# Attention stage of an encoder trunk: projection weights issued from GpSimd's queue, key weights split one unit ahead

## The chip, the cores and the metric

The kernel runs on one core of a Trainium2 chip. The metric is the device time of one execution in microseconds; the time before is the median of three runs, 4154.11 us (4153.01 to 4157.19). A core has TensorE (PE; its weight loads are shown apart as PEld), VectorE (DVE), ScalarE (ACT), GpSimd (POOL) and SyncE (SP). Each engine works through its own list of instructions in order. SyncE, ScalarE and GpSimd can also issue DMA transfers, and a transfer that has to wait for something holds up whatever stands behind it on the engine that issues it.

## The reference

The reference is a trunk of two layers over 1280 tokens (256 of a prompt, 1024 of a sample, the latter a grid of 16 by 64), with 1024 channels. Layer 0 mixes tokens by a bidirectional recurrence, layer 1 by neighbourhood attention, and each is followed by a squared-ReLU MLP. The change acts in layer 1's attention:

```python
qkv = (h @ w_qkv).reshape(B, rows, GRID_W, 3, N_HEADS, HEAD_DIM)
q = _rms_norm(qkv[:, :, :, 0], q_g) * (HEAD_DIM ** -0.5)
k = _rms_norm(qkv[:, :, :, 1], k_g)
v = qkv[:, :, :, 2]
...
s = jnp.einsum('bhcqd,bhrcsd->bhcqrs', q_i, k_s).astype(jnp.float32)
s = s + jnp.transpose(bias, (0, 2, 3, 1, 4)).astype(jnp.float32)
s = jnp.where(col_mask[:, :, None, :], s, -jnp.inf)
p = jax.nn.softmax(s, axis=(-2, -1)).astype(v_s.dtype)
o = jnp.einsum('bhcqrs,bhrcsd->bhcqd', p, v_s)
```

Each query of the grid sees a window of 8 rows and 16 columns around it, with a bias table per head (the random inputs are scaled, which changes nothing in the work done). There are 16 heads of 64 channels.

## The kernel before

All data are 32-bit. To keep precision, each matmul operand is split into a rounded high part and the remainder, and every product is made of three matmuls (`mm3`, lines 96 to 98: high by high, low by high, high by low). `wsplit` (line 81) does this for a weight: a DMA brings a piece into the buffer `raw` (line 89), ScalarE rounds it into `whi` (line 90, a CAST), and GpSimd subtracts to get `wlo` (line 91). For the attention's query and key weights `w_nq` and `w_nk` the piece is half a weight block, 128 partitions by 512 numbers (256 KB), and there is one `raw` buffer for both, so that a half can be fetched only after the half ahead of it has been subtracted. `whi` and `wlo` have two buffers each, one for keys and one for queries in turn.

The attention stage works in eight units m, a unit being 128 channels (two heads). `qk_proj(m)` makes a list of small work items: load the weights, then for keys (which = 1) and queries (which = 0) and for each of three token segments eight `mm3` items, an evacuation from PSUM (`evac`: for queries `sq` and `qf`, lines 1595 and 1597, followed by the casts `qs`), and a tiny matmul for the norm (`nst`, line 1612). The key norm is spread over the tokens by transposes `pb` (line 1647), which take turns with the projections in the two PSUM buffers "ps", so that a `pb` must wait until an earlier result, `qf`, has been evacuated. `attend(m)` gives ten steps of attention, each with three parts: scores on TensorE with the softmax on VectorE, ScalarE and GpSimd (the maximum and reciprocal `mx` at lines 1807 and 1809, the exponential at 1808, the multiply at 1810), transposes `pt` with their copy back (lines 1817 and 1818), and the product with the values (`op`, line 1875).

`attend_all` runs the steps of unit m and spreads the work items of unit m + 1 between them, so that projections fill TensorE while the softmax of a step is under way; unit 0's items are worked off ahead of the first step. TensorE's order is this written order. On the other engines, and on the queues of SyncE and GpSimd, a scheduler fixes the order when the program is built.

Other transfers in the stage: the bias tables `bs` and `bpm` of the next unit (lines 1763 and 1769, SyncE; they wait until VectorE has read the present ones), the values `vs` (line 1752, SyncE; those of unit 0 from GpSimd), and the stores of finished outputs `at_d` (line 1776, GpSimd). At the end `output_operands` loads the first weights `w_no` of the output projection through the same `raw` buffer, from SyncE.

Of the kernel before, what the change touches and what calls it, by code (L numbers as in the profile page):

```python
# [49 lines left out]
class Trunk:  # L50
# [27 lines left out]
        return self.vec[:, base + i:base + i + 1]  # L78


    def wsplit(self, pool, src, n, lo_eng, tag="w", hb=2, rb=2, cuts=1):
        nc = self.nc
        hi = pool.tile([P, n], F32R, name="whi", tag=tag + "h", bufs=hb)
        lo = pool.tile([P, n], F32R, name="wlo", tag=tag + "l", bufs=hb)
        w = n // cuts
        for c in range(0, n, w):
            cs = slice(c, c + w)
            raw = pool.tile([P, w], F32, name="raw", tag=tag + "r", bufs=rb)
            nc.sync.dma_start(raw, src[:, cs])
            nc.scalar.copy(hi[:, cs], raw)  # L90
            lo_eng.tensor_tensor(out=lo[:, cs], in0=raw, in1=hi[:, cs].bitcast(F32), op=ALU.subtract)  # L91
        return hi, lo
# [1464 lines left out]
    def qk_proj(self, m):  # L1557


        nc, a, act = self.nc, self.a, self.act  # L1560
        J = {}
        work = []

        def load():
            for nm in ("ks0", "ks1", "qs0", "qs1", "ql"):
                J[nm] = self.qke[m % 2].tile([P, T], F32R, name=nm, tag=nm, bufs=1)
            for e in range(2):
                J["qs", e], J["ks", e] = J[f"qs{e}"], J[f"ks{e}"]
            J["st"] = self.apn.tile([P, 2, 10, 2], F32, name="nst", tag="nst")
        late = []  # L1570
        for which, wname, g in ((1, "w_nk", self.vec[:, V_KG:V_KG + 1]), (0, "w_nq", self.gq)):
            def wload(wname=wname, which=which):
                J["w", which] = self.wsplit(self.awp, a[wname][m], 1024, nc.gpsimd, rb=1, cuts=2)
            work.insert(1 - which, wload)
            for s, (c0, c1) in enumerate(SEGS):
                n = c1 - c0
                R = {}

                def mm(k, R=R, which=which, n=n, c0=c0, c1=c1):
                    if k == 0:  # L1580
                        R["ps"] = self.apd.tile([P, 512], F32, name="ps", tag="ps")
                    hi, lo = J["w", which]
                    self.mm3(R["ps"][:, :n], hi[:, k * P:(k + 1) * P], lo[:, k * P:(k + 1) * P],
                             act[k][0][:, c0:c1], act[k][1][:, c0:c1], k == 0, k == KT - 1)

                def evac(R=R, which=which, g=g, n=n, c0=c0, c1=c1):
                    ps = R["ps"][:, :n]
                    R["sq"] = self.awk.tile([P, 512], F32, name="sq", tag="sq", bufs=3)
                    sv = R["sq"][:, :n]
                    if which == 0:  # L1590

                        qf = self.awk.tile([P, 512], F32, name="qf", tag="sq", bufs=3)
                        sv = sv.rearrange("p (b r w) -> p r b w", b=4, w=16)
                        ps = ps.rearrange("p (r b w) -> p r b w", b=4, w=16)
                    nc.scalar.activation(sv, ps, AF.Square)
                    if which == 0:
                        nc.scalar.activation(qf[:, :n].rearrange("p (b r w) -> p r b w", b=4, w=16), ps, AF.Copy, scale=g)
                        for e in range(2):
                            es, eo = slice(64 * e, 64 * e + 64), slice(64 - 64 * e, 128 - 64 * e)
                            qe = J["qs", e][:, c0:c1]  # L1600
                            nc.scalar.copy(qe[es], qf[es, :n])
                            nc.vector.tensor_tensor(out=J["ql"][es, c0:c1], in0=qf[es, :n], in1=qe[es].bitcast(F32), op=ALU.subtract)
                            (nc.scalar.copy, nc.vector.tensor_copy)[e](qe[eo], qf[es, :n])
                    else:

                        kh, kl = J["ks1"][:, c0:c1], J["ks0"][:, c0:c1]
                        nc.scalar.activation(kh, ps, AF.Copy, scale=g)
                        nc.vector.scalar_tensor_tensor(out=kl, in0=ps, scalar=g, in1=kh.bitcast(F32), op0=ALU.mult, op1=ALU.subtract)

                def stat(R=R, which=which, n=n, c0=c0):  # L1610
                    for b in range(n // P):
                        nc.tensor.matmul(J["st"][:, which, c0 // P + b, :], R["sq"][:, b * P:(b + 1) * P], self.blk, start=True, stop=True)
                for k in range(KT):
                    work.append(lambda k=k, f=mm: f(k))
                    if k == 2 and late:
                        work.extend(late)
                        late = []
                work.append(evac)
                late.append(stat)
            if which == 1:  # L1620
                def spread(s):
                    c0, c1 = SEGS[s]
                    nb = (c1 - c0) // P
                    re = J["re", s] = self.awk.tile([P, 4, P], F32, name="re", tag="re", bufs=2)
                    rk = J["rs", 1][:, c0 // P:c1 // P, :]
                    nc.vector.tensor_copy(re[:, :nb, :].rearrange("p b (h c) -> p b h c", h=2), rk.unsqueeze(3).to_broadcast([P, nb, 2, 64]))

                def norm(which=which):
                    rs = self.awp.tile([P, 20], F32, name="rs", tag="rs", bufs=4)
                    x = self.awk.tile([P, 40], F32, name="rqx", tag="rqx", bufs=2)  # L1630
                    nc.vector.scalar_tensor_tensor(out=x[:, :20].rearrange("p (b h) -> p b h", h=2), in0=J["st"][:, which], scalar=1.0 / 64,
                                                   in1=self.tn[:, 2 - which].unsqueeze(2).to_broadcast([P, 10, 2]), op0=ALU.mult, op1=ALU.add)
                    self.rsqrt_x(x, self.awk, 20, rs)
                    J["rs", which] = rs.rearrange("p (b h) -> p b h", h=2)
                    if which == 1:
                        spread(0)
                        spread(1)
                late.append(norm)
                kn = norm

        ks = []
        for s, (c0, c1) in enumerate(SEGS):
            def kscale(s=s, c0=c0, c1=c1):
                nb = (c1 - c0) // P
                pb = self.apd.tile([P, 512], F32, name="pb", tag="ps")
                for b in range(nb):
                    nc.tensor.transpose(pb[:, b * P:(b + 1) * P], J["re", s][:, b, :], self.ident)
                if s == 0:
                    spread(2)
                k_ = self.awk.tile([P, 512], F32, name="kf", tag="sq", bufs=3)[:, :c1 - c0]  # L1650
                nc.vector.tensor_tensor(out=k_, in0=J["ks1"][:, c0:c1].bitcast(F32), in1=J["ks0"][:, c0:c1].bitcast(F32), op=ALU.add)
                nc.vector.tensor_tensor(out=k_, in0=k_, in1=pb[:, :c1 - c0], op=ALU.mult)

                for e in range(2):
                    es, eo = slice(64 * e, 64 * e + 64), slice(64 - 64 * e, 128 - 64 * e)
                    ke = J["ks", e][:, c0:c1]
                    nc.scalar.copy(ke[es], k_[es])
                    nc.gpsimd.tensor_tensor(out=ke[eo], in0=k_[es], in1=ke[es].bitcast(F32), op=ALU.subtract)
            ks.append(kscale)
        work.insert(2, load)  # L1660
        n = len(work)
        for i, f in enumerate(ks):
            work.insert(n - 17 + 5 * i, f)
        work += [lambda: None] * 2 + late + [lambda: kn(0)]
        return J, work
# [295 lines left out]
```

## Time and profile before

| | |
|---|---|
| median of 3 runs | 4154.11 us (4153.01 to 4157.19) |
| profiled execution | 4156.58 us, span 4154.6 us |
| mean granted TensorE clock | 0.957 |
| the stage's units, between 2675.5 and 3071.5 us | six, 62.2 to 69.1 us each |
| TensorE busy in these six | 363.0 of 396.0 us |
| GpSimd busy in these six | 173.7 of 396.0 us |

In rows of the trace, "out<-in" names what an instruction writes and reads, and the brackets at a row's end give the idle time of the engine ahead of it and what ended it. "ACT whi L90" is the instruction of line 90 on ScalarE that writes `whi`. A row of waits reads: who waited for whom, the sum in us, how many times, the longest. For a DMA the row with three numbers gives minimum, median and maximum. SPq is SyncE's queue.

### The profile page before, as it was taken

The page shows a single profiled execution, that of the slowest core. Times are in us where ns is not written, and L with a number is a line of the kernel's source. Part 1 is how long each engine was busy: PE and PEld are TensorE (multiplying, and loading weights), DVE is VectorE, ACT ScalarE, POOL GpSimd, SP SyncE. Part 2 cuts the span into 40 slices and gives each one's busy share as a digit, 9 for nine tenths or more (in the row PEclk, how much of TensorE's full clock was granted, in tenths as well). Part 3 has the DMA queues.
Part 4 walks back from the last instruction along what each step waited for, and adds up shares of the span by engine and source line. Part 5 has one row for each costly group of instructions (what it writes and reads, how often), then busy time and mean ns, then how long its engine had stood idle before and what let it go on. Part 6 is the DMA issues. An engine that isn't in the chain of part 4 may idle for free.

```text
span 4154.6 us, 86991 instructions
## 1 busy us (share of the span) xinstructions
PE 3837.0 (92%) x35188; PEld 3233.9 (78%) x35188; DVE 2459.8 (59%) x4771; ACT 1547.9 (37%) x3731; POOL 1262.3 (30%) x1210
## 2 busy tenths in 40 slices
PE   7897879688889799999999989899989999999999
PEld 4664669688888688888888879777767788888887
DVE  7888973466666447555555560566664655555555
ACT  6776651354555431111111132555554211112111
POOL 5440000123323434222222240344453422222222
PEclk9997889899999899999999999999999999999999
DMA  3325555866765331111111125333343111111101
GB/s 111 89 95 203 195 189 151 203 175 176 184 172 139 122 114 36 32 41 41 37 36 41 41 73 169 73 84 73 69 117 129 47 41 41 36 36 41 41 31 61
DMA packets 385794, 393.22 MB, mean 95 GB/s; under 512 B 161872, under 2 KB 306480, under 8 KB 384112
## 3 DMA queue, kind: packets, MB, share of 16 engines
q1 hardware_dynamic: 331760, 315.16, 27.1%
q10 hardware_dynamic: 46704, 61.35, 4.3%
q0 software_dynamic: 6928, 11.15, 1.0%
q8 instruction: 276, 4.52, 0.5%
q14 instruction: 126, 1.03, 0.1%
HBM read 277.54 MB, written 121.24 MB: 96 GB/s over the span
## 4 chain that ended last, share of the span: by engine, by line
PE 72%; DVE 13%; issue 4%; ACT 4%; DMA 4%; POOL 2%; SPq 1%; ACTq 0%; DVEq 0%; POOLq 0%
PE ps L96 17%; PE ps L97 17%; PE ps L98 17%; PE by L998 3%; PE bx L998 3%; PE kps L960 2%; PE vps L512 1%; PE vps L513 1%; PE vps L514 1%; PE zps L1166 1%; PE op L1875 1%; DVE cs L628 1%; PE pt L1817 1%; PE aps L833 1%; PE yps L922 1%
## 5 line engine op out<-in xcount | busy, mean ns | idle before, releaser
L1432 DVE TENSOR_TENSOR x<-ps,x 128x256 f32<-128x256 f32 x1488 | 813.6, 594 | 638.8 <-PE ps L98 638.3
L96 PE MATMUL ps<-ah,whi 128*128 128x512 f32 (+1 forms) x2304 | 846.6, 367 | 5.5 <-ACT whi L90 5.0
L98 PE MATMUL ps<-ah,wlo 128*128 128x512 f32 (+1 forms) x2304 | 826.8, 359 | 2.5 <-POOL wlo L91 2.3
L97 PE MATMUL ps<-al,whi 128*128 128x512 f32 (+1 forms) x2304 | 826.7, 359 | 0.0
L91 POOL TENSOR_TENSOR wlo<-raw,whi 128x1024 fp32r<-128x1024 f32 (+1 forms) x178 | 390.6, 2195 | 864.3 <-ACT whi L90 836.8
L96 PE MATMUL ps<-hh,whi 128*128 128x512 f32 (+1 forms) x1536 | 547.7, 357 | 14.3 <-DVE x L1432 14.3
L97 PE MATMUL ps<-hl,whi 128*128 128x512 f32 (+1 forms) x1536 | 545.9, 355 | 0.0
L98 PE MATMUL ps<-hh,wlo 128*128 128x512 f32 (+1 forms) x1536 | 545.9, 355 | 0.0
L96 PEld LDWEIGHTS ps<-ah,whi 128*128 128x128 f32 x2304 | 437.4, 190 | 84.7 <-issue 13.0
L98 PEld LDWEIGHTS ps<-ah,wlo 128*128 128x128 f32 x2304 | 436.6, 189 | 73.9 <-POOL wlo L91 3.4
L97 PEld LDWEIGHTS ps<-al,whi 128*128 128x128 f32 x2304 | 437.2, 190 | 65.4 <-issue 1.1
L90 ACT CAST whi<-raw 128x1024 fp32r<-128x1024 f32 (+1 forms) x206 | 200.6, 974 | 712.7 <-PE ps L97 640.5
L96 PEld LDWEIGHTS ps<-hh,whi 128*128 128x128 f32 x1536 | 291.2, 190 | 59.2 <-DVE x L1432 17.4
L1411 POOL TENSOR_TENSOR rl<-rl 128x512 f32<-128x512 f32 (+1 forms) x192 | 173.9, 906 | 504.0 <-PE ps L98 463.3
L98 PEld LDWEIGHTS ps<-hh,wlo 128*128 128x128 f32 x1536 | 291.4, 190 | 41.8
L97 PEld LDWEIGHTS ps<-hl,whi 128*128 128x128 f32 x1536 | 291.4, 190 | 40.9
L1410 ACT ACTIVATE rl<-ps 128x512 f32<-128x512 f32 (+1 forms) x192 | 100.4, 523 | 547.9 <-PE ps L98 547.9
L965 DVE TENSOR_TENSOR zz<-kps,cst 128x512 f32<-128x512 f32 x160 | 110.3, 690 | 207.7 <-ACT ll L970 207.6
L1413 ACT CAST hh<-rl 128x512 fp32r<-128x512 f32 (+1 forms) x192 | 105.5, 549 | 321.3 <-POOL rl L1411 321.2
L1414 DVE TENSOR_TENSOR hl<-rl,hh 128x512 fp32r<-128x512 f32 (+1 forms) x192 | 119.3, 621 | 150.2 <-ACT hh L1413 149.9
L1810 POOL TENSOR_TENSOR s<-s,mx 128x384 f32<-128x384 f32 (+1 forms) x154 | 116.8, 769 | 212.6 <-DVE mx L1809 148.1
L960 PE MATMUL kps<-x 64*64 64x128 f32 (+1 forms) x2560 | 167.9, 320 | 13.2 <-issue 12.1
(313 smaller groups left out, 7869.0 us busy)
## 6 DMA issues: line engine op xcount, KB each, us to landing
x<-x_d SPq DMA_DIRECT2D x88, 512.0 KB, 4.5
raw<-in_w_down_dram SPq DMA_DIRECT2D x64, 512.0 KB, 3.5
raw<-in_w_up_dram SPq DMA_DIRECT2D x64, 512.0 KB, 3.5
eab<-x_d SPq DMA_DIRECT2D x80, 256.0 KB, 6.0
x_d<-ar ACTq DMA_DIRECT2D x32, 512.0 KB, 3.3
x_d<-bk ACTq DMA_DIRECT2D x32, 512.0 KB, 4.3
bs<-tab SPq DMA_DIRECT2D x128, 96.0 KB, 3.7
v_d<-vt ACTq DMA_DIRECT2D x80, 128.0 KB, 3.7
```

What stands on the lines that cost most here:

```text
L90: nc.scalar.copy(hi[:, cs], raw)
L91: lo_eng.tensor_tensor(out=lo[:, cs], in0=raw, in1=hi[:, cs].bitcast(F32), op=ALU.subtract)
L96: mm(ps, sh, mh, start=first, stop=False)
L97: mm(ps, sh, ml, start=False, stop=False)
L98: mm(ps, sl, mh, start=False, stop=last)
L960: mm(J["kp"][out, e, 192 * c + 192 - w:192 * c + 192], x[es, b, 2 * pr + c], x[es, 5 - w // 64:5, 2 * pr + c], start=True, stop=True)
L965: nc.vector.tensor_tensor(out=z, in0=src[:, :, :, :P], in1=self.mask[d].unsqueeze(1).unsqueeze(1).to_broadcast([P, 2, 2, P]), op=ALU.mult)
L998: mm = lambda out, a, b, start, stop: nc.tensor.matmul(out, a, b, start=start, stop=stop, skip_group_check=True)
L1411: nc.gpsimd.tensor_tensor(out=r[:, :n], in0=r[:, :n], in1=r[:, :n], op=ALU.mult)
L1414: nc.vector.tensor_tensor(out=hl[:, :n], in0=r[:, :n], in1=hh[:, :n].bitcast(F32), op=ALU.subtract)
L1432: nc.vector.tensor_tensor(out=xv, in0=ps[:, :n], in1=xv, op=ALU.add)
L1810: nc.gpsimd.tensor_tensor(out=s[:, :nk], in0=s[:, :nk], in1=mx[:, 2:3].to_broadcast([P, nk]), op=ALU.mult)
```

## The change

`wsplit` gets an argument for the engine that issues its transfers. In `qk_proj` the key and query weights of units 1 to 7 come from GpSimd's queue; unit 0's stay on SyncE. The key weights of unit m + 1 become an item of unit m's list, between its key and its query projections (`wnext`), and unit m takes the pair made there. The query weights of units 1 to 7 are loaded behind the first four key matmul items instead of at the list's start, and the allocation of the unit's tiles (`load`) moves to the front of the list.

```diff
-    def wsplit(self, pool, src, n, lo_eng, tag="w", hb=2, rb=2, cuts=1):
+    def wsplit(self, pool, src, n, lo_eng, tag="w", hb=2, rb=2, cuts=1, dma=None):
...
-            nc.sync.dma_start(raw, src[:, cs])
+            (dma or nc.sync).dma_start(raw, src[:, cs])
...
-            def wload(wname=wname, which=which):
-                J["w", which] = self.wsplit(self.awp, a[wname][m], 1024, nc.gpsimd, rb=1, cuts=2)
-            work.insert(1 - which, wload)
+            def wload(wname=wname, which=which, m=m):
+                J["w", which] = self.wsplit(self.awp, a[wname][m], 1024, nc.gpsimd, rb=1, cuts=2, dma=nc.gpsimd if m else None)
+
+            def wnext():
+                self.wnext = self.wsplit(self.awp, a["w_nk"][m + 1], 1024, nc.gpsimd, rb=1, cuts=2, dma=nc.gpsimd)
+            if m == 0:
+                work.insert(1 - which, wload)
+            elif which == 1:
+                J["w", 1] = self.wnext
+            else:
+                work.insert(4, wload)
+            if which == 0 and m < 7:
+                work.append(wnext)
...
-        work.insert(2, load)
+        work.insert(0 if m else 2, load)
```

The order of the instructions moves at three places. On SyncE's queue, in one unit of the stage, before (a row with a count stands for so many alike; the numbers behind `bs` tell its two tables apart):

```order
L89 DMA raw<-in_w_nq_dram 128x512
L1769 DMA bpm<-tab 16x2x128 x16
L89 DMA raw<-in_w_nk_dram 128x512
L1763 DMA bs_29465<-tab 16x6x256 x8
L1752 DMA vs<-vs_d 128x4x128
```

The first row is the second half of the queries; the key half stood behind the sixteen bias transfers. These weight rows are gone from SyncE's queue. On GpSimd's list the same weights now stand as follows (lines of the changed kernel: 1820 is the softmax multiply, 1786 the output store, 1668 the scaled keys):

```order
L1820 TENSOR_TENSOR s<-s,mx 128x384 x2
L91 TENSOR_TENSOR wlo<-raw,whi 128x512
L89 DMA raw<-in_w_nq_dram 128x512
L1820 TENSOR_TENSOR s<-s,mx 128x384 x2
L91 TENSOR_TENSOR wlo<-raw,whi 128x512
L89 DMA raw<-in_w_nk_dram 128x512
L1820 TENSOR_TENSOR s<-s,mx 128x128 x2
L1820 TENSOR_TENSOR s<-s,mx 128x384
L1786 DMA at_d<-ot 128x512
L1820 TENSOR_TENSOR s<-s,mx 128x384 x3
L1820 TENSOR_TENSOR s<-s,mx 128x128 x2
L91 TENSOR_TENSOR wlo<-raw,whi 128x512
```

Each load follows the subtraction that frees the buffer, so the first half of the next weight is issued well ahead of its use; the second halves have one softmax step between issue and use. On ScalarE, in the middle of a unit behind the last key projection, before (1192 and 1193 are the key norm):

```order
L1595 ACTIVATE sq<-ps 128x512
L1607 ACTIVATE ks_30858<-ps,vec 128x512
L1818 COPY s<-pt 128x128 x2
L1808 ACTIVATE s,mx<-s,mx 128x384 x2
L1192 ACTIVATE rqt<-rqx 128x20
L1193 ACTIVATE rs<-rqt 128x20
L90 CAST whi<-raw 128x512
L1818 COPY s<-pt 128x384
```

And now:

```order
L90 CAST whi<-raw 128x512
L1605 ACTIVATE sq<-ps 128x512
L1617 ACTIVATE ks_30848<-ps,vec 128x512
L1828 COPY s<-pt 128x128 x2
L1818 ACTIVATE s,mx<-s,mx 128x384 x2
L90 CAST whi<-raw 128x512
L1192 ACTIVATE rqt<-rqx 128x20
L1193 ACTIVATE rs<-rqt 128x20
```

Both casts are of the next unit's key halves; the second came behind the norm and was of a first half. At the unit's end a cast of the query half now stands ahead of the casts `qs`, and the copy `s<-pt` that stood ahead of them comes behind the last exponentials.

## The prediction

> **What bounds the kernel now.** I read the page's first part, then the waits of TensorE in the attention stage (2640 to 3075 us, where the change acts), then the stage cut into its units of work, then the rows around each wait.
>
> ```profile
> PE 3837.0 (92%) x35188; PEld 3233.9 (78%) x35188; DVE 2459.8 (59%) x4771; ACT 1547.9 (37%) x3731; POOL 1262.3 (30%) x1210
> ```
>
> TensorE is the bound, so a transfer matters only if TensorE stands still for it. Its waits in the stage, summed:
>
> ```profile
> PE pb L1647 <- ACT qf L1597: 14.5, 11, 3.9
> PE pt L1817 <- POOL s L1810: 10.8, 6, 1.8
> PE ps L96 <- ACT whi L90: 4.2, 1, 4.2
> PE ps L98 <- POOL wlo L91: 1.3, 1, 1.3
> ```
>
> Only the last two name the weights (5.5 us). The first is a wait for ScalarE's evacuation qf, which frees the PSUM buffer that the transposes pb need; the question is why ScalarE is late. Six stretches, each from the second group of pb of one unit to that of the next, hold the same work (398 or 399 matmul rows):
>
> ```profile
> 2675.50:2744.60 69.10, 60.53 (x399) 46.94 (x399) 41.36 (x104) 37.35 (x97) 30.61 (x35) 0.95 0.36 79
> 2744.60:2806.80 62.20, 59.22 (x398) 45.91 (x398) 42.13 (x104) 35.81 (x94) 27.98 (x33) 0.97 0.35 75
> 2806.80:2873.90 67.10, 60.77 (x399) 47.25 (x399) 41.05 (x103) 36.30 (x96) 29.59 (x34) 0.95 0.34 73
> 2873.90:2941.10 67.20, 62.66 (x399) 48.49 (x399) 41.04 (x104) 36.20 (x96) 29.18 (x35) 0.92 0.33 74
> 2941.10:3006.60 65.50, 59.78 (x398) 46.07 (x398) 40.15 (x104) 36.09 (x95) 27.80 (x33) 0.97 0.37 75
> 3006.60:3071.50 64.90, 60.04 (x399) 46.19 (x399) 40.83 (x104) 36.21 (x96) 28.51 (x34) 0.97 0.33 76
> ```
>
> (Columns: stretch, length, busy PE, PEld, DVE, ACT, POOL, then the granted clock.) One unit takes 62.2 us, the others up to 69.1. The long first one holds the 4.16 and 1.32 us for weights, the last four one wait each for qf; the short one has neither:
>
> ```profile
> 2700.76 0.53 PE L96 MATMUL ps<-ah,whi 128*128 128x256 f32 x1 [4.16 <-ACT whi L90]
> 2797.77 0.44 PE L1647 MATMUL pb<-cst,re 128*128 128x128 f32 x2
> 2863.86 0.44 PE L1647 MATMUL pb<-cst,re 128*128 128x128 f32 x2 [3.86 <-ACT qf L1597]
> 2929.47 0.66 PE L1647 MATMUL pb<-cst,re 128*128 128x128 f32 x2 [2.12 <-ACT qf L1597]
> 2996.62 0.44 PE L1647 MATMUL pb<-cst,re 128*128 128x128 f32 x2 [2.65 <-ACT qf L1597]
> 3061.44 0.44 PE L1647 MATMUL pb<-cst,re 128*128 128x128 f32 x2 [1.75 <-ACT qf L1597]
> ```
>
> Why qf is late is seen on ScalarE and on SyncE's queue. In the short unit ScalarE's cast of the next key half starts without a wait; in the next unit it waits 6.54 us for the transfer, and qf, two rows of exponentials later, slips with it:
>
> ```profile
> 2791.84 0.60 ACT L90 CAST whi<-raw 128x512 fp32r<-128x512 f32 x1
> 2796.43 0.46 ACT L1597 ACTIVATE qf<-ps,gq 128x256 f32<-128x256 f32 x1
> ...
> 2849.95 0.62 ACT L90 CAST whi<-raw 128x512 fp32r<-128x512 f32 x1 [4.20 <-DMA raw<-in_w_nq_dram]
> 2860.59 0.62 ACT L90 CAST whi<-raw 128x512 fp32r<-128x512 f32 x1 [6.54 <-DMA raw<-in_w_nk_dram]
> 2863.33 0.48 ACT L1597 ACTIVATE qf<-ps,gq 128x256 f32<-128x256 f32 x1
> ```
>
> ```profile
> 2847.25 0.34 SPq L89 DMA_DIRECT2D raw<-in_w_nq_dram  x1
> 2847.68 8.67 SPq L1769 DMA_DIRECT2D bpm<-tab  x16
> 2856.45 0.37 SPq L89 DMA_DIRECT2D raw<-in_w_nk_dram  x1
> ```
>
> The key half stands behind sixteen bias transfers that occupy the queue for 8.67 us, and those behind the query half, which waited for the only raw buffer. From the short unit to this one the cast slipped by 2860.59 - 2791.84 = 68.75 us and qf by 66.90, against a unit of 62.2: 4.7 us late, of which TensorE felt 3.86. So ScalarE has some 0.9 us of slack there (in the short unit qf ends at 2796.89, pb starts at 2797.77).
>
> **The change part by part.** *The transfers leave SyncE's queue for GpSimd's.* Four halves a unit (256 KB each) are issued by GpSimd, each right behind the subtraction that frees the raw buffer. The nearest row for the issue is the output store: same queue, same engine, same 128x512 tile.
>
> ```profile
> L1776 POOL DMA_DIRECT2D at_d<-ot x14: 581/581/598, 2682.2 to 3100.8; - x14
> DMA to landing us min/median/max: 2.3/4.1/6.7
> ...
> L1752 POOL DMA_DIRECT2D vs<-vs_d x2: 775/1004/1233, 2600.5 to 2601.8; - x2
> DMA to landing us min/median/max: 8.0/8.2/8.5
> ...
> DMA to landing us min/median/max: 2.7/2.7/2.9
> ```
>
> (The last row is SyncE's own query load.) Issue: 4 x 0.58 = 2.3 us of GpSimd a unit, which is busy 28 of 62 us. What would pay, if it stood there, is the softmax multiply at the unit's end, for which TensorE waits 1.80 us; but GpSimd is idle 4.50 us before that multiply, so I cost the issues at nothing:
>
> ```profile
> 2822.42 1.61 POOL L1810 TENSOR_TENSOR s<-s,mx 128x384 f32<-128x384 f32 x2 [4.50 <-DVE rqx L1631]
> 2823.30 0.55 PE L1817 MATMUL pt<-cst,s 128*128 128x128 f32 x3 [1.80 <-POOL s L1810]
> ```
>
> Landing: between 2.3 and 8.5 us. I take 2.3 to 4.1, since the store has the size and shape of the loads, and the 8 us belong to a pair of transfers cut into 512-byte pieces, one of 1 MB. Three of the four halves have room: both first halves are issued a third of a unit or more ahead. The tight one is the second half of the keys.
>
> *The next unit's keys in the middle of this one.* In the new order ScalarE casts the first half behind the last key matmul, then evacuates, and two exponentials later casts the second half. On the short unit's clock:
>
> ```profile
> 2787.16 0.60 ACT L1595 ACTIVATE sq<-ps 128x512 f32<-128x512 f32 x1 [3.51 <-PE ps L98]
> 2790.20 0.60 ACT L1808 ACTIVATE s<-s,mx 128x384 f32<-128x384 f32 x1
> 2793.87 0.86 ACT L1818 COPY s<-pt 128x384 f32<-128x384 f32 x2 [1.43 <-POOL wlo L91]
> 2792.52 1.29 POOL L91 TENSOR_TENSOR wlo<-raw,whi 128x512 fp32r<-128x512 f32 x1
> ```
>
> First cast from 2787.16 (0.60), subtraction to 2789.05 (1.29), second load landed at 2791.4 to 2793.2, ScalarE free for it from 2790.9: it waits 0.5 to 2.3 us. Cast and the two tiny norm steps then end at 2792.5 to 2794.3, against the copy that started at 2793.87 anyway. Late by 0 to 0.4 us, under the slack of 0.9; I take 0.2 a unit, +1.2. VectorE waits for the norm step there and the exponentials for VectorE, which is why I don't take zero.
>
> *What is gained.* Unit by unit against 62.2: 6.9 + 0 + 4.9 + 5.0 + 3.3 + 2.7 = 22.8 us. The waits alone are 4.16 + 1.32 + 3.86 + 2.12 + 2.65 + 1.75 = 15.9; the other 6.9 is the slow pace of TensorE behind each wait. After the 2.12 us the 512-column matmuls start 0.43 us apart, elsewhere 0.24:
>
> ```profile
> 2931.21 0.63 PE L97 MATMUL ps<-al,whi 128*128 128x512 f32 x1
> 2931.64 0.63 PE L98 MATMUL ps<-ah,wlo 128*128 128x512 f32 x1
> ...
> 2868.45 0.40 PE L97 MATMUL ps<-al,whi 128*128 128x512 f32 x1
> 2868.69 0.40 PE L98 MATMUL ps<-ah,wlo 128*128 128x512 f32 x1
> ```
>
> So a microsecond of wait costs 22.8 / 15.9 = 1.43. The Trainium skill, "TensorE: Matmul & The Clock Gate", section "What's actually happening", says that the clock falls to half only after an idle window of about 3.4 us. By that only the waits of 4.16 and 3.86 would carry a penalty; the gain would be an estimated 19 instead of 22.8, and the 2.12 us row speaks against it.
>
> *Smaller moves.* The list of TensorE's work shifts: one key matmul triple now stands ahead of the transposes that wait 1.80 us, and ScalarE's query casts come ahead of a copy, so that the last exponentials start earlier. Bounds: 0 to 1.8 us in six units. I take 0.35 each, about one triple, -2. At the stage's start GpSimd and ScalarE do the second key half in a row ahead of the first unit's scaled keys, and a cast of 0.60 us comes ahead of the query statistics: between -0.6 (a cast leaves the way of the scaled keys) and +4.1 (one landing waited for in full), I take +0.6, the one cast. At the end the first output weights stay on SyncE, their first cast moves behind qf, and the second joins ScalarE's batch of output casts: between -0.6 and +2.7 (a landing from SyncE), I take +1. SyncE's bias transfers start up to 5 us earlier; nobody waits for them.
>
> Sum: -22.8 - 2 + 1.2 + 0.6 + 1 = -22. The profiled execution took 4156.58 us (span 4154.6 and 2.0 around it), 2.5 above the median of 4154.11; from the median I get **4132**.
>
> **The rivals.** *Late landing (slower).* With a landing of L the copy is late by L - 3.8 and TensorE waits L - 4.7, times 1.43, six times. At 7.2 us this eats the gain; at the 8.3 us of GpSimd's own earlier loads it is 5.2 a unit, +31, and 31 - 22 gives 4163. For it speaks that row, and the store's maximum of 6.7 us beside a 1 MB load; against it that the middle of a unit has no such load. The Trainium skill, "SBUF — State Buffer", section "Summary: rules for kernel authors", advises against this very move: descriptors of GpSimd's transfers are starved while VectorE runs its two-port modes. Its example (about 0.6 us becoming 3.1) would add an estimated 2.5 us to a landing; the 21 stores issued in this stage show 0.58 us each at the issue, with a spread of landing that could hide it.
>
> *GpSimd in the way.* A subtraction of 1.29 and an issue of 0.58 could land ahead of the multiply at the unit's end: 1.87 x 1.43 x 6 = +16, giving 4148. The 4.50 us of idle time speak against it.
>
> *The late transfer was not the cause of qf.* If qf stays late for another reason, only the 5.5 us for weights go, times 1.43: 4146. Against it stands the short unit, which has all but the wait.
>
> **How the numbers follow.** The forecast has 0.64 (4122, if the 1.80 us waits shrink by half with their slow pace, to 4140), the late landing 0.15, GpSimd in the way 0.11, another cause 0.10. A measurement tells some 0.2% (8.3 us) from no change, so 4145.8 divides faster from same: the forecast and most of the last rival's spread below 4146 give 0.72 faster, the rest of both middle rivals 0.13, the late landing 0.15 slower. The range 4122 to 4152 leaves out the late landing and the extremes.
>
> **What would show it.** Right: the four waits of pb for qf and the 4.16 us gone or under 0.5, units of 61 to 63 us, ScalarE waiting under 2.5 us for key or query loads. The landing step is wrong if raw loads from GpSimd take over 5 us; the cost step if the 1.80 us wait has grown. The forecast fails if units stay above 65 us.

## The result and the profile after

The changed kernel takes 4131.12 us (median of six runs, 4125.86 to 4135.41); the kernel before, run beside it, 4156.06 us. The ratio is 0.9936, with a 95% interval of 0.9923 to 0.995: 25 us faster (21 to 32), where the prediction said 22. The profiled execution took 4126.86 us (span 4125.1); the one before had a span of 4154.6, so the two traces differ by 29.5 us.

TensorE's waits in the attention stage of the changed kernel (2640 to 3075 us), summed as before:

```profile
PE s L1809 <- DVE s L1844: 6.1, 3, 5.1
PE pb L1657 <- ACT qf L1607: 5.8, 7, 1.1
PE pt L1827 <- ACT rs L1193: 4.2, 6, 0.8
PE pt L1827 <- POOL s L1820: 3.5, 7, 0.5
PE pb L1657 <- DVE mx L1819: 2.7, 5, 0.5
```

(Lines have moved by ten: `pb` is now L1657, `qf` L1607, `pt` L1827.) No wait names `whi` or `wlo`. The waits for `qf` were 14.5 us with a longest of 3.9, now 5.8 with 1.1; the 5.1 us belongs to the stage's end. The 1.80 us at each unit's end has become two short waits:

```profile
2753.10 0.52 PE L1827 MATMUL pt<-cst,s 128*128 128x128 f32 x3 [0.77 <-ACT rs L1193]
2754.05 0.55 PE L1827 MATMUL pt<-cst,s 128*128 128x128 f32 x3 [0.43 <-POOL s L1820]
```

The six units, cut at the second group of `pb` as before (first and last, and behind them the stage's end):

```profile
2676.53:2737.13 60.60, 57.92 (x399) 44.59 (x399) 42.19 (x104) 36.02 (x96) 32.20 (x38) 1.00 0.35 81
...
2979.80:3039.84 60.04, 57.77 (x398) 44.74 (x398) 42.41 (x105) 35.43 (x95) 28.77 (x35) 1.00 0.33 73
3039.84:4125.10 1085.26, 1056.81 (x5527) 890.22 (x5527) 599.72 (x1067) 252.08 (x437) 338.88 (x248) 0.99 0.18 55
```

All six lie between 60.04 and 60.98 us and sum to 363.3, against 396.0: 32.7 us less. All six in one, before and now:

```profile
2675.50:3071.48 395.98, 362.98 (x2389) 280.83 (x2389) 246.54 (x618) 217.94 (x571) 173.64 (x200) 0.96 0.35 75
2676.53:3039.84 363.31, 348.07 (x2388) 267.75 (x2388) 251.03 (x619) 215.35 (x570) 189.69 (x220) 1.00 0.36 80
```

The units are shorter than the shortest of before (62.2), which the prediction had taken as the floor, and the granted clock (the third number from the end) is 1.00 in each, where no unit of before had more than 0.97. TensorE's busy time in the six fell from 363.0 to 348.1 us for the same matmuls, its idle time from 33.0 to 15.3. So, in these two traces, 14.9 us of the gain are clock and 17.8 us are waits.

ScalarE's waits for weights between 2665 and 3045 us, and GpSimd's issues there with the landing of all 21 (minimum, median, maximum):

```profile
ACT whi L90 <- DMA raw<-in_w_nq_dram: 10.9, 6, 2.2
ACT whi L90 <- DMA raw<-in_w_nk_dram: 3.7, 5, 1.0
```

```profile
L89 POOL DMA_DIRECT2D raw<-in_w_nq_dram x11: 577/582/585, 2690.2 to 2993.5; - x11
L89 POOL DMA_DIRECT2D raw<-in_w_nk_dram x10: 577/581/585, 2696.5 to 2961.7; - x10
...
DMA to landing us min/median/max: 2.8/4.0/5.1
```

Before, ScalarE waited up to 4.4 us for query and 6.5 us for key halves.

### The profile page after: what moved, and what is told of

It is laid out like the page before. It is cut to its first block, busy times and chain, and to the rows that moved or that the text cites. A ratio compares the mean times of both kernels' runs of the same rounds, so it can differ in the third digit from the quotient of the medians.

```text
span 4125.1 us, 86973 instructions
## 1 busy us (share of the span) xinstructions
PE 3823.1 (93%) x35188; PEld 3215.7 (78%) x35188; DVE 2468.4 (60%) x4771; ACT 1545.1 (37%) x3731; POOL 1284.6 (31%) x1238
## 4 chain that ended last, share of the span: by engine, by line
PE 74%; DVE 12%; issue 4%; DMA 3%; ACT 3%; POOL 2%; SPq 0%; ACTq 0%; DVEq 0%; POOLq 0%
PE ps L96 18%; PE ps L97 17%; PE ps L98 17%; PE by L998 3%; PE bx L998 3%; PE kps L960 2%; PE vps L512 1%; PE vps L513 1%; PE vps L514 1%; PE op L1885 1%; PE zps L1166 1%; PE aps L833 1%; PE yps L922 1%; DVE mu L187 1%; PE pt L1827 1%
## 5 line engine op out<-in xcount | busy, mean ns | idle before, releaser
L97 PEld LDWEIGHTS ps<-al,whi 128*128 128x128 f32 x2304 | 433.9, 188 | 64.9 <-issue 1.1
L960 PE MATMUL kps<-x 64*64 64x128 f32 (+1 forms) x2560 | 164.4, 313 | 14.1 <-issue 11.6
```

The lines of the kernel that those rows point to most:

```text
L97: mm(ps, sh, ml, start=False, stop=False)
L960: mm(J["kp"][out, e, 192 * c + 192 - w:192 * c + 192], x[es, b, 2 * pr + c], x[es, 5 - w // 64:5, 2 * pr + c], start=True, stop=True)
```

## Where the clock fell

The windows that show the granted clock can be laid as finely as one likes. In quarter microseconds TensorE runs at 1.00 or at 0.50, with values between only in a piece that holds a change, and every stretch at 0.50 lasts 3.41 us or a multiple, so it loses 1.71 us or a multiple. In one execution the starts lie on one grid: in the kernel before at 2636.00, 2700.75, 2762.25, 2823.50, 2864.50, 2892.00, 2929.50, 2997.75 and 3062.50 us, which are 0, 18.97, 36.99, 54.93, 66.94, 75.00, 85.99, 105.98 and 124.95 times 3.413 us from the first. Laid in hundredths, the windows give the edges themselves (one stretch runs from 2823.73 to 2827.14 us). Two places of the kernel before, each with a wait of 1.80 us at a unit's end, in windows on that grid (length, busy time of PE, PEld, DVE, ACT, POOL, clock):

```profile
2820.32:2823.73 3.41, 1.61 (x15) 0.98 (x11) 2.11 (x8) 3.31 (x9) 1.31 (x2) 1.00 0.99 169
2823.73:2827.14 3.41, 3.17 (x21) 2.83 (x21) 3.14 (x7) 1.69 (x5) 1.60 (x2) 0.50 0.56 73
2953.44:2956.85 3.41, 2.26 (x22) 1.59 (x21) 2.65 (x8) 2.89 (x7) 0.23 (x1) 1.00 0.59 117
2956.85:2960.26 3.41, 2.52 (x24) 1.99 (x24) 2.77 (x5) 2.62 (x8) 2.68 (x3) 1.00 1.01 119
```

In the first pair the wait falls into one window, TensorE is idle for 1.80 us of it, and the next window runs at half clock. In the second the same wait straddles the boundary, neither window has more than 1.15 us idle, and the clock stays. So the price of a wait is its length, and 1.71 us more if enough idle time falls into one window. In the six units ten windows of the kernel before ran at half clock (two of the eight stretches are double), and none of the changed kernel.

The fourteen traces of the table below, taken together between 2665 and 3040 us, give the odds, with each trace's grid taken from its own edges: of windows at full clock with 1.7 us or more idle, 19 of 20 were followed by a window at half clock; with 1.35 to 1.7 us, 4 of 20; with 0.9 to 1.35 us, 5 of 69; with less, none of 1397. There is no sharp threshold in the idle time that the trace shows (1.20 us brought the clock down and 1.72 us did not), so what the chip counts is not exactly that.

## The experiments

Each is compared with the kernel before, run beside it: 4152.06 us beside e1, e2, e3 and e5, 4154.69 beside e4 and e6, 4155.71 beside e9, e10, e11 and after_again. Across these groups compare the ratios, not the times. "Six units" are the stretches between the second groups of `pb`, in one profiled execution, and the last column counts windows at half clock in them.

| kernel | median us | ratio to before (95%) | six units us | half clock |
|---|---|---|---|---|
| before | 4156.06 | | 396.0 | 10 |
| changed | 4131.12 | 0.9936 (0.9923 to 0.995) | 363.3 | 0 |
| e1_queue | 4129.68 | 0.9946 (0.9934 to 0.9957) | 368.3 | 4 |
| e2_place | 4132.83 | 0.9959 (0.9947 to 0.9972) | 375.3 | 1 |
| e3_qfirst | 4131.00 | 0.9954 (0.9942 to 0.9967) | 369.3 | 3 |
| e5_wno | 4129.19 | 0.9942 (0.993 to 0.9954) | 365.8 | 2 |
| e4_act2 | 4128.52 | 0.9939 (0.9925 to 0.9952) | 362.0 | 0 |
| e4_act4 | 4135.55 | 0.9956 (0.9942 to 0.997) | 367.2 | 0 |
| e4_act8 | 4136.76 | 0.9956 (0.9942 to 0.9969) | 367.5 | 1 |
| e6_raw2 | 4126.55 | 0.9927 (0.9914 to 0.9941) | 365.1 | 1 |
| e9_long | 4157.66 | 1.0006 (0.9996 to 1.0017) | 391.3 | 8 |
| e11_before_raw2 | 4149.02 | 0.9979 (0.9967 to 0.9992) | 385.8 | 0 |
| e10_best | 4127.91 | 0.9927 (0.9913 to 0.9941) | 365.6 | 3 |
| after_again | 4129.64 | 0.9931 (0.9917 to 0.9946) | 364.3 | 0 |

### The queue alone, the place alone

e1_queue is the kernel before with GpSimd as the issuer; e2_place is the changed kernel with SyncE as the issuer.

```diff
-                J["w", which] = self.wsplit(self.awp, a[wname][m], 1024, nc.gpsimd, rb=1, cuts=2)
+                J["w", which] = self.wsplit(self.awp, a[wname][m], 1024, nc.gpsimd, rb=1, cuts=2, dma=nc.gpsimd if m else None)
             work.insert(1 - which, wload)
```

> The kernel before with only the queue changed: the four halves of key and query weights of units 2 to 8 are issued by GpSimd, every load stays at its old place in the list. If the cause was SyncE's queue (weights standing behind bias transfers of 8.67 us), nearly the whole gain comes: units of 60.5 to 62.5 us, no wait of TensorE for qf above 0.5 us behind a late cast, 4131 to 4138 us. If it was the place (keys a unit ahead), the loads still come too late: the 4.16 us wait for whi and at least two of the four waits for qf stay, 4143 to 4152 us.

```diff
-                ... rb=1, cuts=2, dma=nc.gpsimd if m else None)
+                ... rb=1, cuts=2, dma=None)
...
-                self.wnext = ... rb=1, cuts=2, dma=nc.gpsimd)
+                self.wnext = ... rb=1, cuts=2)
```

> The changed kernel with every weight load back on SyncE, at its new place. Theory (queue): weights again stand behind bias transfers, ScalarE waits 4 us or more for some key or query halves, and units of 63 to 67 us come back: 4140 to 4155 us. Rival (place alone suffices): loads have a third of a unit or more of room, SyncE's transfers land in time, units stay at 60.6 us: 4129 to 4135 us.

The theory was right on e1_queue, the rival on e2_place by its time: 4129.68 and 4132.83 us. Either half of the change takes the long waits away; TensorE's longest is 1.2 us in e1_queue and 1.5 in e2_place. The place does it less well in the trace, where the six units of e2_place take 12 us more than those of the changed kernel. In e1_queue ScalarE still waits for loads, but for 2.0 us at most where it was 6.5. Its waits, and two neighbouring units of it:

```profile
ACT whi L90 <- DMA raw<-in_w_nq_dram: 10.6, 6, 2.0
ACT whi L90 <- DMA raw<-in_w_nk_dram: 6.8, 5, 1.6
```

```profile
2672.56:2732.87 60.31, 57.58 (x398) 44.72 (x398) 41.39 (x104) 36.32 (x96) 32.07 (x38) 1.00 0.37 82
2732.87:2794.40 61.53, 58.88 (x398) 46.00 (x399) 41.34 (x104) 35.91 (x96) 32.05 (x38) 0.97 0.35 80
```

The two units have the same waits of TensorE; the second is 1.2 us longer, and TensorE is 1.3 us longer busy in it, for one window at half clock. In e2_place weights do stand behind bias transfers, as the theory said. On SyncE's queue a key half comes behind sixteen of them:

```profile
2704.82 0.34 SPq L89 DMA_DIRECT2D raw<-in_w_nq_dram  x1
2705.26 7.58 SPq L1779 DMA_DIRECT2D bpm<-tab  x16
2712.94 0.37 SPq L89 DMA_DIRECT2D raw<-in_w_nk_dram  x1
```

ScalarE waits for it only in this unit (2.1 us, and 4.0 us for the query half ahead; the unit takes 64.35 us). In all six it waits 4.4 us for key halves and 4.0 us for query halves.

What follows: lateness of the weights was the cause, and the queue and the place are two cures for it, not two parts of a sum. Three other units of e2_place take 62.3 to 62.5 us at a clock of 1.00, with 3.9 to 4.1 us idle where the changed kernel has 2.7; which order of work makes that, the runs do not separate.

### Weights in time by a second buffer

If lateness is the cause, a second raw buffer in the kernel before should cure it as well, with neither the queue nor the place changed.

```diff
-                J["w", which] = self.wsplit(self.awp, a[wname][m], 1024, nc.gpsimd, rb=1, cuts=2)
+                J["w", which] = self.wsplit(self.awp, a[wname][m], 1024, nc.gpsimd, rb=2, cuts=2)
```

(and the same for `w_no`, which shares the buffer.)

> The kernel before with two raw buffers in place of one for these weights, nothing else: SyncE can then issue both halves without waiting for a subtraction in between, and the bias transfers no longer come between them. If this wait for the only buffer was what made the weights late, the 4.16 us wait and the four waits for qf go, while the waits of 1.80 us at the unit's end stay: units of 60.7 to 62.3 us, 4132 to 4138 us. If SyncE's queue is late in any case (bias transfers of 8.67 us ahead of both halves), two or more of the waits stay: 4143 to 4152 us.

It was 4149.02 us, by the number the second case, but for a reason that neither named. The weights came in time: ScalarE waits for none of them, and the long waits for `qf` are gone. Yet five of the six units take 64.9 us, at full clock, with new waits of TensorE in each. The waits between 2665 and 3045 us, and one of these units:

```profile
PE pt L1817 <- POOL s L1810: 9.5, 6, 1.8
PE pb L1647 <- DVE mx L1809: 8.9, 5, 2.1
PE s L1799 <- DVE s L1834: 8.7, 11, 1.2
```

```profile
2800.59:2865.47 64.88, 58.22 (x398) 44.83 (x399) 44.82 (x104) 36.28 (x96) 29.22 (x34) 1.00 0.35 76
```

VectorE is late here, and its busy time has grown from 42.2 (the short unit of before) to 44.8 us. The instruction that grew is one cast, first in this kernel, then in the kernel before; behind them GpSimd's row at the same time in this kernel:

```profile
2853.46 3.69 DVE L1603 CAST qs<-qf 64x256 fp32r<-64x256 f32 x1
```

```profile
2735.02 1.23 DVE L1603 CAST qs<-qf 64x256 fp32r<-64x256 f32 x1
```

```profile
2854.48 2.52 POOL L91 TENSOR_TENSOR wlo<-raw,whi 128x512 fp32r<-128x512 f32 x2
```

With both halves in SBUF GpSimd does the two subtractions back to back, until 2857.00, and the cast ends at 2857.15. All five units of 64.9 us hold such a cast, of 3.69 or 3.70 us; in the first of the six it took 1.22 us, and that unit is the short one:

```profile
2674.32:2735.70 61.38, 57.85 (x399) 44.80 (x399) 43.29 (x105) 36.38 (x96) 29.77 (x34) 1.00 0.35 80
```

With one raw buffer a load stands between them. The Trainium skill, "SBUF — State Buffer", section "Summary: rules for kernel authors", says that a VectorE instruction in a two-port mode and a GpSimd instruction block each other, whichever comes second waiting for the first. The times of these rows agree (3.69 us against 1.23), except that the cast waited through several GpSimd instructions, not one. That these 2.5 us make most of the 3.5 us between the units fits the wait of 2.1 us for VectorE and the short unit; they were not taken away by themselves, so this is argued, not shown.

### The order at the unit's end

e3_qfirst puts the query load back to the head of the list.

```diff
-                work.insert(4, wload)
+                work.insert(0, wload)
```

> The changed kernel with the query weights' load moved back to the head of the unit's list (it stood four items later). Question: where do the 10 us come from by which units fell below the short unit of before (60.6 against 62.2). If the order of TensorE's and ScalarE's work at the unit's end is the cause (a key matmul triple ahead of the transposes that waited 1.80 us), part or all of the 1.6 us per unit returns: 4134 to 4141 us with a wait of pt of 1.5 us or more in each unit. If the gain only follows from the weights being in time, nothing changes: 4129 to 4133 us.

The time (4131.00 us) cannot be told from the changed kernel's. In the trace the wait of `pt` at the unit's end is 1.24 to 1.32 us in each unit in place of about 0.7, and three of the six units have a window at half clock. That is part of the way back that the first case expected, 6 us in this trace (369.3 against 363.3), within what the comparison of times leaves open.

### A delay on ScalarE: two, four, eight casts

```diff
                 self.wnext = self.wsplit(...)
+                if m:
+                    for i in range(4):
+                        z = self.awp.tile([P, 512], F32R, name="zz", tag="zz", bufs=1)
+                        nc.scalar.copy(z, self.wnext[0][:, 512:1024].bitcast(F32))
```

> The changed kernel with two casts of 128x512 (0.62 us each in its trace) added to ScalarE in the middle of six units, between the exponentials and the second key half; nobody reads their result, the work is only added. In the changed kernel qf ends 1.5 us before TensorE takes pb (2726.1 against 2727.66 us), so 1.2 us of delay should cost nothing: both theories of the price of a wait give 0 to 2 us over the changed kernel. With the prediction's slack of 0.9 us it would be 0.3 x 1.43 x 6 = 2.6 us.

> The same with four such casts (2.4 us). TensorE should then wait 2.4 - 1.5 = 0.9 us for qf in each of six units. At the prediction's price of 1.43 us for each us of wait this is +8 us; if a wait costs its own length, and 1.71 us more only where TensorE stands idle for most of one 3.41-us window of the clock, +5 us, with the clock of these units still at 1.00. With no slack at all it would be 2.4 x 1.43 x 6 = +21 us.

> The same with eight such casts (4.8 us), so waits for qf of 3.3 us in six units. At 1.43 us per us of wait: +28 us over the changed kernel. By windows of the clock: 3.3 us of wait and one or two windows at half clock (1.71 us each) in every unit, +30 to +40 us; the stretches at half clock should each start on one grid of 3.41 us and each lose 1.71 us or a multiple of it, whatever the length of the wait.

Two casts cost nothing, as expected. Four gave waits of 1.5 to 1.6 us (for VectorE's `kf`, which is late in turn) at a clock of 1.00 throughout, and 3.9 us in the six units, 3.7 of them idle time of TensorE. In the trace that is nearer to the second theory's 5 than to 8; the times cannot tell the two apart (4135.55 us is 7.0 above the kernel with two casts). Eight casts missed every expectation: 5 us of work a unit, and TensorE's longest wait for `qf` is 1.4 us:

```profile
PE pb L1661 <- ACT qf L1611: 11.1, 13, 1.4
```

ScalarE's rows show why. The cast of the second key half and `qf` behind it, in the changed kernel and with the eight casts:

```profile
2721.86 0.62 ACT L90 CAST whi<-raw 128x512 fp32r<-128x512 f32 x1 [0.77 <-DMA raw<-in_w_nk_dram]
2725.63 0.48 ACT L1607 ACTIVATE qf<-ps,gq 128x256 f32<-128x256 f32 x1
```

```profile
2722.45 0.62 ACT L90 CAST whi<-raw 128x512 fp32r<-128x512 f32 x1 [0.75 <-DMA raw<-in_w_nk_dram]
2729.09 0.48 ACT L1611 ACTIVATE qf<-ps,gq 128x256 f32<-128x256 f32 x1
```

Seven of the eight casts stand between these rows, spread among exponentials and copies, and part of them fills gaps in which ScalarE waited: the stretch to the end of `qf` grows from 4.25 to 7.12 us, by 2.9 and not by the 4.3 of seven casts. In the changed kernel `qf` ends 1.55 us before TensorE takes `pb` (2727.66 us). What is left, 1.3 us, is the wait that TensorE has there (1.28). So these three runs do not test a long wait.

### A long wait on purpose

e9_long forces the delay: a chain in which each copy reads the one before, and `qf` takes its scale from the last.

```diff
                     nc.scalar.activation(sv, ps, AF.Square)
+                    if which == 0 and n == 256 and 0 < m < 7:
+                        z = [self.awk.tile([P, 257], F32, name="zz", tag=f"zz{i}", bufs=1) for i in range(2)]
+                        nc.scalar.copy(z[0][:, 256:], g)
+                        nc.scalar.copy(z[0][:, :256], R["sq"][:, :256])
+                        for i in range(9):
+                            nc.scalar.copy(z[1 - i % 2], z[i % 2])
+                        g = z[1][:, 256:]
```

> The changed kernel, in whose six units the clock of TensorE never fell, with a chain of ten copies of 128x256 on ScalarE ahead of qf in the middle of each of six units (each reads what the one before wrote, the last hands qf its scale; the work is only added). At 0.28 to 0.4 us each and two exponentials that slip with them, against the slack of 1.5 us, TensorE should wait 1.5 to 3.5 us for qf in each unit. If a wait is dear only where TensorE idles for more than about 1.5 us of one 3.41-us window, then stretches at half clock appear now, one or two a unit, each losing 1.71 us: the units grow by the wait and 1.71 to 3.4 us more, +20 to +40 us over the changed kernel. If the slow pace behind the waits of the kernel before came from something else (the late weights themselves), the units grow by the wait alone, with the clock at 1.00: +9 to +21 us.

TensorE waits 4.14 us in six units (five of them among the six stretches of the table, one ahead of them), longer than either case assumed, and the half-clock windows are there: one or two behind each wait, on one grid again. One of the waits, the grid's windows around it, and the units with this wait and the next:

```profile
2869.95 0.44 PE L1664 MATMUL pb<-cst,re 128*128 128x128 f32 x2 [4.14 <-ACT qf L1614]
```

```profile
2867.36:2870.77 3.41, 0.82 (x7) 0.82 (x8) 2.03 (x7) 3.23 (x10) 1.78 (x2) 1.00 0.83 136
2870.77:2874.18 3.41, 3.41 (x12) 2.84 (x12) 1.93 (x5) 2.07 (x5) 1.36 (x2) 0.51 0.00 0
```

```profile
2814.60:2879.99 65.39, 59.57 (x398) 45.90 (x399) 40.58 (x104) 40.02 (x107) 31.19 (x38) 0.97 0.34 75
2879.99:2947.31 67.32, 61.40 (x398) 47.04 (x399) 40.55 (x104) 40.30 (x107) 31.22 (x38) 0.95 0.34 73
```

The unit with one such window takes 65.4 us, that with two 67.3, for the same wait of 4.14 us. Worked out from the unit of the changed kernel: 60.6 + 4.14, less 0.52 and 0.46 for shorter waits that fall away or shrink behind it, plus 1.71 or 3.42, gives 65.5 or 67.2. The time is 28.0 us above the changed kernel beside it (4157.66 against 4129.64). That lies in the range of 20 to 40, but since the wait came out longer than assumed, the total alone decides little: the six waits by themselves would give 6 x (4.14 - 0.98) = 19 us. The split decides. The six stretches of the traces have grown by 28.0 us (391.3 against 363.3), and 11.6 of them are busy time of TensorE for the same matmuls (359.7 against 348.1). The weights are as much in time as in the changed kernel (ScalarE waits 1.0 us for key halves and 2.4 for query halves at most), so the slow pace comes from the wait and not from the weights.

### The small moves

```diff
-            self.wo.append(self.wsplit(self.awp, self.a["w_no"][m], 1024, nc.gpsimd, rb=1, cuts=2))
+            self.wo.append(self.wsplit(self.awp, self.a["w_no"][m], 1024, nc.gpsimd, rb=1, cuts=2, dma=nc.gpsimd))
```

> The changed kernel with the first output weights (w_no), too, issued by GpSimd. In the tail of the changed kernel a store tile waits 7.12 us (5.59 before) and ScalarE 3.18 us for a load of the attention output that SyncE issued last. If the tail's 2 us of loss come from the SyncE queue there, they return and up to 2 more: 4127 to 4130 us, and the stretch from the last pb group to the end falls from 1085.3 to 1081 to 1083.5 us. If they come from the order of ScalarE's casts, no change: 4130 to 4133 us.

The stretch from the last `pb` to the end is 1081.0 us, against 1085.3 and 1085.8 in two executions of the changed kernel, as expected at best; the time, 4129.19 us, cannot be told from it. But the move is not shown to be the reason. The stretch in this kernel, and in e10_best, which has the same move (and two buffers):

```profile
3046.40:4127.40 1081.00, 1053.73 (x5527) 887.90 (x5527) 600.08 (x1070) 251.88 (x436) 336.32 (x248) 0.99 0.17 55
3034.53:4122.40 1087.87, 1055.43 (x5527) 889.72 (x5527) 600.99 (x1070) 251.49 (x436) 336.03 (x247) 0.99 0.17 54
```

Of the 4.3 us under the changed kernel 3.1 are busy time of TensorE for the same matmuls (1056.8 there), which is clock, and in e10_best the stretch is longer than in the changed kernel.

e6_raw2 is the changed kernel with `rb=2` for the three weights; e10_best has that and the move of e5_wno.

> The changed kernel with two raw buffers in place of one, so that a second half need not wait until the subtraction has read the first. ScalarE's waits for loads (10.9 us for query and 3.7 us for key halves in six units, longest 2.2) should go. If the landing of the second key half still held TensorE up, 2 to 5 us come back; if, as the slack of 1.5 us says, it does not, the time stays within 2 us of the changed kernel.

> The changed kernel with two raw buffers and the first output weights issued by GpSimd: both edits that looked better than the changed kernel in one profile. Units of 60.06 us in place of 60.6 (-3 us in the stage) and a tail of 1081 in place of 1085 us would make 4124 us; if both were only the scatter of single executions, it equals the changed kernel beside it within 2 us.

> The changed kernel once more, beside the two above: 4129 to 4133 us. If the clock of 1.00 in all six units is a property of its short waits, it comes again; if it was the luck of one execution, stretches at half clock show in some of the six units.

With two buffers ScalarE waits for none of these loads any more, and the first four units of either kernel take 60.04 to 60.09 us in place of 60.6 to 61.0, some half a microsecond less. Whether the waits for second halves cost that is open: e4_act2, which has one buffer and waits as long (0.9 us for key halves, 2.5 for query halves at most), begins with units of 60.1 to 60.3 us too. What all three lack is the changed kernel's waits of `pb` for VectorE's `mx`. The two units behind the four are longer. This one of e10_best has two windows at half clock and a wait of 1.65 us that the changed kernel does not have:

```profile
2909.21:2973.80 64.59, 61.12 (x398) 47.10 (x399) 43.55 (x104) 36.05 (x96) 31.64 (x38) 0.95 0.33 76
```

Beside each other the changed kernel has 0.9931 and e10_best 0.9927: no difference that can be told. The changed kernel's second trace has a clock of 1.00 in all six units again, so that is its waits and not luck. No version clearly beats it.

## Why the prediction was right, and where it was off

**The cause.** Right, and its signs came: the four waits of `pb` for a late `qf` and the 4.16 us are gone, and ScalarE waits 2.2 us at most for a load. Only the units fell outside the 61 to 63 us named, on the short side. The weights were late behind bias transfers, ScalarE slipped and `qf` with it. e1_queue, which changes nothing but the issuer, removes the long waits; the rival that `qf` was late for another reason is out.

**The transfers on GpSimd.** Issue: taken as 0.58 us each and hidden; measured 0.58, and TensorE's waits of `pt` for GpSimd fell from 10.8 to 3.5 us. Landing: taken as 2.3 to 4.1 us, measured 2.8 to 5.1, median 4.0. The tight one, the second key half, landed in 2.9 to 3.3 us in all five units; the 5.1, just over the 5 us named as a sign of failing, is a query half, which has room. The late landing that would have made the kernel slower did not come. The Trainium skill's warning ("SBUF — State Buffer", section "Summary: rules for kernel authors") that GpSimd's descriptors are starved beside VectorE does not show in these 21 issues of 577 to 585 ns; whether it has a part in the spread of the landings (SyncE's took 2.7 to 2.9 us) the runs do not tell.

**The second key half.** Taken: ScalarE waits 0.5 to 2.3 us, cost 0.2 a unit. Measured: at most 1.0 for keys and 2.2 for queries. What that cost is not shown: e6_raw2's first units would put it at 0.5 a unit, 3 us in place of 1.2, but e4_act2 has units as short with the waits in place.

**The gain of 22.8 us.** This is the term that was mis-sized. Its floor was the shortest unit, 62.2 us, read as a unit without the fault. The row quoted for it had a clock of 0.97, and it holds one window at half clock (from 2762.25 us) behind the 1.80 us wait that ends at 2761.03 us. Clean units take 60.6 us, so the whole is 32.7, not 22.8 and 2. Split by the two totals, the waits gave 17.8 us where 15.9 and 2 were predicted, which agrees, and the clock 14.9 where 6.9 was. The multiplier of 1.43 is not a rate: beside waits of 1.5 us at full clock the units grew by idle time alone (e4_act4), and waits of 4.14 us their length and one or two quanta of 1.71 us (e9_long).

**The rule on the clock.** The Trainium skill, "TensorE: Matmul & The Clock Gate", section "What's actually happening", gives a free-running window of about 3.4 us and two states. The grid of 3.413 us and the clocks of 1.00 and 0.50 agree. That a whole idle window is needed does not: 1.80 us of 3.41 were enough. The prediction kept the row and not the rule, which was right.

**The wait at the unit's end, -2.** The wait itself gave 0.6 us a unit (1.80 to 0.77 and 0.43), 3.6 in six, of which new waits of 0.5 us for VectorE in five units took most back. What was missed is that at 1.80 us it was long enough to bring the clock down, in three units of six, and that the two short pieces of the changed kernel are not. In e3_qfirst, where the first piece is 1.24 to 1.32 us, three of the six units have a window at half clock again.

**Start and end.** Start: +0.6 predicted, +0.3 measured (54.92 to 55.25 us for the stretch of the first unit, both at a clock of 0.97; 56.66 at 0.91 in the second trace of the changed kernel). End: +1 predicted, +2.1 measured (1083.1 to 1085.3), inside its bounds, but not by the mechanism named. The stretch in the kernel before:

```profile
3071.48:4154.60 1083.12, 1053.06 (x5527) 887.29 (x5527) 598.59 (x1068) 252.17 (x437) 339.75 (x248) 0.99 0.17 55
```

Beside the changed kernel's row TensorE's busy time grew by 3.8 us for the same matmuls and its idle time fell by 1.6. Counted by their edges, 9.4 windows ran at half clock there and 6.9 before. So the +2.1 is clock, and no longer waiting shows in it.

**The sum.** Worked in the traces: -32.7 + 0.3 + 2.1, and 0.7 in the unchanged part ahead, gives -29.6, against -22 predicted: in the traces the forecast is some 8 us short. The medians differ by 25 us, with an interval of 21 to 32, so the range and the way were right by the mechanism, and that the time came within 1 us of the forecast is luck. Single traces are a rough measure of the whole: the stretch up to the first unit, which the kernels hardly differ in, took 2608 to 2624 us in the fourteen.

## What to carry to other kernels

Before a "clean" repetition of a stage is taken as the floor, look at its granted clock: at 0.97 it is not clean, and a repetition at 1.00 may be shorter than any that the profile shows. In this kernel a wait of TensorE cost its length, and mostly 1.71 us more for each clock window that it left half empty, so cutting a wait of 1.8 us in two can be worth more than the time it saves. And where a load is late, an earlier place, another queue or another buffer may each cure it, but ask of each where the work that follows the load will then stand.

## What the runs showed of the hardware

The clock moves in whole windows of 3.41 us, on a grid that runs on through an execution whatever TensorE does, and 1.2 to 1.7 us idle in a window may or may not bring it down. A unit of almost exactly 19 windows (64.88 us in e11_before_raw2, 19.01 times 3.413) meets the grid at nearly the same phase every time: there the five waits of 1.80 us never brought the clock down, though they left 1.58 to 1.72 us of a window idle.

A VectorE instruction can last several times its usual length while GpSimd works: the cast of 64x256 3.69 us in place of 1.23, and in e6_raw2 an operation on 128x20 numbers 1.96 us in place of 0.17, ending within 0.1 us of GpSimd's multiply. VectorE's row and GpSimd's:

```profile
2965.97 1.96 DVE L1195 SCALAR_TENSOR_TENSOR rqt<-rqt,rqx 128x20 f32<-128x20 f32 x1
```

```profile
2966.27 1.61 POOL L1820 TENSOR_TENSOR s<-s,mx 128x384 f32<-128x384 f32 x2
```
